# Latent attention by pairs of heads: keys and weighted values of two heads side by side in the array, weights scaled before their transposes

## The chip, the core and the metric

The kernel runs on one core of a Trainium2 chip. Five engines work there from instruction queues of their own: TensorE (PE in the profile, its weight loads PEld), VectorE (DVE), ScalarE (ACT), GpSimd (POOL) and SyncE (SP), which here only issues transfers. The metric is the device time of one launch in microseconds, as the median of several runs. Below, a *bank* is one of the 8 parts of PSUM, the memory that TensorE writes its products to; each holds 512 float32 columns on 128 partitions.

## The reference, cut to what matters

The model has two layers over 256 context tokens and 512 latent tokens of width 1024. Each layer joins three mixers (mLSTM, RWKV-7 and latent attention), projects their output, adds, normalises, and ends in a large lookup of single-neuron experts (PEER). Only the latent attention and the output projection are touched:

```python
def _mla_prep(p, q_norm_g, q_up, kv_norm_g, kv_up, ang):
    cq, ckv, k_rope = _split(p, [384, 256, 32])
    q  = (_rms(cq, q_norm_g) @ q_up).reshape(b, t, 6, 96)        # 64 plain + 32 rotary
    kv = (_rms(ckv, kv_norm_g) @ kv_up).reshape(b, t, 6, 128)    # 64 key + 64 value
    ...                                                          # rotary part, shared by the heads
    return concat([q_nope, q_rope]), concat([k_nope, k_rope]), v

def _attend(q, k, v):
    s = einsum('bqhd,bkhd->bhqk', q, k) * MLA_SCALE
    pr = softmax(s, axis=-1)
    return einsum('bhqk,bkhd->bqhd', pr, v)
```

Latent queries attend to all 768 tokens, context queries to the 256 context tokens; in the last layer context queries are not needed. Then `y = concat([mlstm, rwkv, attention]) @ w_out`.

## The kernel before

Tokens are handled in 6 tiles of 128: tiles 0 and 1 are context, 2 to 5 latent. A plain float32 `nc.tensor.matmul` shows in the trace as two weight loads and two matmuls; the projections use three float32r products of high and low halves instead (`PASSES`).

*Order.* The program is written as Python generators. `weave` advances two or three of them in proportion to given numbers of steps; `flight(units, 3, 2)` keeps up to three units alive, starts a new one every second round, and advances the oldest first. From the order so written and from estimates of its own, the tile framework fixes one list of instructions for each engine before the run. An instruction may be moved ahead of earlier ones on its engine when its inputs are estimated to be there sooner. All tiles from `self.bank()` share one ring of 8 banks.

*Around the attention.* `mixer` first runs `project_mla` (compressed queries `cq` and keys `ckv`, the sums for their norms, and the rotary part of the keys). Then it weaves `mla` (84 steps) with `project_mlstm` (44 steps), whose matmuls are L446 (`fm`, called for each feature tile) and L530. After that come mLSTM and the RWKV projections, then RWKV (whose `tile_prep` has L893), then `project_out`, which is the first step of `peer`.

*`mla`, L744 to L836.* First `rk`, the norm of the keys spread over 64 partitions (L753, L754). Then for each of 6 heads the keys: for both token spans (256 and 512 columns) two accumulated matmuls with 64 weight columns (L760) and a multiplication by `rk` on DVE into `kT` (L761); and for each of 6 token tiles the values `vM` (L764, L765). Then the units: `queries(h)` projects one head's queries for all tokens (L784 to L788, whose last step is on POOL). `unit(h, t)` is one head and one tile of queries, in four steps: scores per span (L799) and their maximum (L800); negated scaled maximum (L804, L805), exponentials with their sums (L809), sum and reciprocal (L811, L812); transposes of the weights (L818) and their copies to SBUF (L820 on DVE, L822 on ACT); weighted values (L826: weights as the stationary operand, the 64 value columns moving), evicted by ACT with the reciprocal as scale (L827). With `need` (layer 0) there are 36 units, 12 of them context tiles over 256 keys; in layer 1 there are 24. With head 5 the row block of a tile goes to DRAM (L829).

*`project_out`, L1198 to L1243.* For each token tile the 1024 features of `y` are loaded, transposed in two groups of four (L1228), and split into high and low halves (L1231 on ACT, L1232 on DVE) for the product with `w_out` (L1239).

Of the kernel before, what the change touches and what calls it, by code (L numbers as in the profile page):

```python
# [20 lines left out]
AF = mybir.ActivationFunctionType  # L21
ALU = mybir.AluOpType
# [6 lines left out]
NT = 6  # L29
NTOK = 768  # L30
# [179 lines left out]
class Net:  # L210
# [533 lines left out]
    def mla(self, p, o):  # L744
# [1 line left out]
        up = self.param(p, l, ("k_up", [128, 2, 384]), ("v_up", [128, 2, 384]))  # L746
        kup, vup = up["k_up"], up["v_up"]

        rk = self.t(p, [64, NTOK], "rk")
        for c, n in TSPANS:  # L750
            ps = self.bank()
            for t in range(n // 128):
                nc.tensor.matmul(ps[:64, t * 128:(t + 1) * 128], lhsT=o["rms"][:, 1, c // 128 + t:c // 128 + t + 1].to_broadcast([128, 64]), rhs=self.ident, start=True, stop=True)  # L753
            nc.scalar.activation(out=rk[:, c:c + n], in_=ps[:64, :n], func=AF.Copy)  # L754
        yield
        for h in range(6):
            for c, n in TSPANS:
                ps = self.bank()
                for i in range(2):
                    nc.tensor.matmul(ps[:64, :n], lhsT=kup[:, i, h * 64:(h + 1) * 64], rhs=o["ckv"][:, i, c:c + n], start=i == 0, stop=i == 1)  # L760
                nc.vector.tensor_tensor(out=self.kT[0:64, h, c:c + n], in0=ps[:64, :n], in1=rk[:, c:c + n], op=ALU.mult)  # L761
            ps = self.bank()
            for i in range(2):
                nc.tensor.matmul(ps[:, :384], lhsT=o["ckv"][:, i, h * 128:(h + 1) * 128], rhs=vup[:, i, :], start=i == 0, stop=i == 1)  # L764
            nc.scalar.activation(out=self.vM[:, h, :], in_=ps[:, :384], func=AF.Copy, scale=o["rms"][:, 1, h:h + 1])  # L765
            yield
        sc = self.t(p, [128, NT], "srq")
        nc.vector.tensor_scalar_mul(out=sc, in0=o["rms"][:, 0, :], scalar1=MLA_SCALE)
        qTs = {}
        yM = self.t(p, [128, NT, 384], "yM")  # L770

        def queries(h):
            qT = self.t(p, [96, NTOK], "qT", 2)
            t1 = self.t(p, [128, NTOK], "rt", 2)
            t2 = self.t(p, [128, NTOK], "rt", 2)
            qup = self.t(p, [128, 3, 128], "q_up", 2)
            nc.sync.dma_start(out=qup, in_=a["q_up"][l, :, :, h * 128:(h + 1) * 128])
            for c, n in TSPANS:
                if c == 0 and not self.need:
                    continue  # L780
                cs = slice(c, c + n)
                ps = self.bank()
                for i in range(3):
                    nc.tensor.matmul(ps[:, :n], lhsT=qup[:, i, :], rhs=o["cq"][:, i, cs], start=i == 0, stop=i == 2)  # L784
                nc.scalar.activation(out=qT[0:64, cs], in_=ps[0:64, :n], func=AF.Copy)
                nc.vector.tensor_tensor(out=t1[64:96, cs], in0=ps[64:96, :n], in1=self.rope[64:96, cs], op=ALU.mult)
                nc.vector.tensor_tensor(out=t2[64:96, cs], in0=ps[96:128, :n], in1=self.rope[96:128, cs], op=ALU.mult)
                nc.gpsimd.tensor_tensor(out=qT[64:96, cs], in0=t1[64:96, cs], in1=t2[64:96, cs], op=ALU.add)  # L788
            qTs[h] = qT
            yield  # L790

        def unit(h, t):
# [17 lines left out]
            if len(spans) == 2:  # L810
                nc.vector.tensor_tensor(out=sm[:, 0:1], in0=sm[:, 0:1], in1=sm[:, 1:2], op=ALU.add)  # L811
            nc.vector.reciprocal(out=sm[:, 0:1], in_=sm[:, 0:1])  # L812
            yield
            pT = self.t(p, [128, NTOK], "pT", 2)
            for c0, w in spans:
                ps = self.bank()
                for i in range(0, w, 128):
# [3 lines left out]
                else:  # L821
                    nc.scalar.activation(out=pT[:, c0:c0 + w], in_=ps[:, :w], func=AF.Copy)  # L822
            yield
            po = self.bank()
            for i in range(nk):
                nc.tensor.matmul(po[:, :64], lhsT=pT[:, i * 128:(i + 1) * 128], rhs=self.vM[:, i, h * 64:(h + 1) * 64], start=i == 0, stop=i == nk - 1)  # L826
            nc.scalar.activation(out=yM[:, t, h * 64:(h + 1) * 64], in_=po[:, :64], func=AF.Copy, scale=sm[:, 0:1])  # L827
            if h == 5:
                nc.sync.dma_start(out=self.y[t * 128:(t + 1) * 128, 640:1024], in_=yM[:, t, :])  # L829

        units = [queries(0)]
        for h in range(6):
            units += [unit(h, t) for t in range(0 if self.need else CT, NT)]
            if h < 5:
                units.insert(len(units) - 2, queries(h + 1))
        yield from self.flight(units, 3, 2)  # L836


# [359 lines left out]
    def project_out(self, p, pw, l, need, xk, hold):  # L1198
# [18 lines left out]
        for s, tiles in streams:  # L1217
            gate = self.gate_rows(p, l, 2, s, f"gate{s}")
            for t in tiles:
# [2 lines left out]
                if left:  # L1222
                    ahead.append(load())
                yT = [self.t(p, [128, 8, 128], f"yT{i}", 2, F32R) for i in range(2)]
                for g in range(2):
                    ps = self.bank()
                    for k in range(4):
                        nc.tensor.transpose(ps[:, k * 128:(k + 1) * 128], y[:, (g * 4 + k) * 128:(g * 4 + k + 1) * 128], self.ident)  # L1228
                    ps = ps.rearrange("p (k n) -> p k n", k=4)
                    hi, lo = (z[:, g * 4:g * 4 + 4, :] for z in yT)  # L1230
                    nc.scalar.activation(out=hi, in_=ps, func=AF.Copy)  # L1231
                    nc.vector.tensor_tensor(out=lo, in0=ps, in1=hi.bitcast(F32), op=ALU.subtract)  # L1232
                z = self.t(p, [128, D], "z", 1)
# [537 lines left out]
```

## Time and profile before

| | |
|---|---|
| median of 3 runs | 5154.06 us (5148.3 to 5161.02) |
| the profiled execution | 5153.65 us, of which its span 5151.7 us |
| busy share of the span | PE 89%, PEld 75%, DVE 71%, POOL 40%, ACT 36% |
| granted TensorE clock, mean | 0.941 of full speed |
| DMA, mean | 192 GB/s |

Rows of the profile read as follows. L818 is line 818 of the kernel. A timeline row gives the start in us from the span's start, how long the instruction or run of like instructions lasted, the engine, the line, the operation, the tile written and those read, and shapes; a bracket at its end tells how long the engine sat idle before it and what it then waited for. A run of matmuls counts from the first start to the last end; matmuls are pipelined, so the next may start before that end. [...]

### The profile page before, as it was taken

What the parts mean: (1) busy time and instruction counts of PE and PEld (TensorE: products, weight loads), DVE (VectorE), ACT (ScalarE), POOL (GpSimd) and SP (SyncE); (2) the same over time, 40 slices, a digit from 0 to 9 for tenths busy, and PEclk for the clock granted to TensorE, in tenths of its full rate; (3) what the DMA queues carried; (4) which work ended last, traced back from release to release, by engine and by line L of the source; (5) the groups of instructions that cost most, each with busy time, mean ns of one, the idle gap of its engine ahead of it and who ended that gap; (6) DMA issues with size and microseconds to landing.
All of it is one profiled execution on the core that took longest, in us unless ns stands there. A gap on an engine that the chain in (4) does not pass through costs nothing.

```text
span 5151.7 us, 89696 instructions
## 1 busy us (share of the span) xinstructions
PE 4604.4 (89%) x35473; PEld 3857.8 (75%) x35473; DVE 3676.4 (71%) x7469; ACT 1848.1 (36%) x3330; POOL 2065.0 (40%) x1761
## 2 busy tenths in 40 slices
PE   6998888888987999999999689978778889999998
PEld 4675567667876887778878467767667888988887
DVE  4444455679885999999999734545579757777777
ACT  2342255232553222222222223345433543333332
POOL 1102333244773555555555210233336634444442
PEclk9998889999998999999999898989989999999999
DMA  4016400321477999999999310100222578999994
GB/s 144 22 43 220 159 4 5 122 83 56 170 284 255 352 342 329 347 342 343 346 335 339 104 34 23 45 22 3 85 96 91 214 269 311 320 316 316 315 319 173
DMA packets 402933, 991.60 MB, mean 192 GB/s; under 512 B 35104, under 2 KB 167584, under 8 KB 401744
## 3 DMA queue, kind: packets, MB, share of 16 engines
q1 hardware_dynamic: 289552, 574.91, 32.2%
q0 software_dynamic: 112960, 410.96, 22.1%
q8 instruction: 279, 4.57, 0.4%
q14 instruction: 142, 1.16, 0.1%
HBM read 894.45 MB, written 91.19 MB: 191 GB/s over the span
## 4 chain that ended last, share of the span: by engine, by line
PE 64%; DVE 15%; POOL 6%; DMA 5%; issue 5%; ACT 4%; SPq 1%; POOLq 0%; DVEq 0%; ACTq 0%
PE acc L1564 17%; PE A L1497 15%; PE b L446 6%; PE b L1355 4%; PE spill L1564 3%; PE b L1497 2%; PE b L1239 2%; DMA c<-early 1%; PE b L799 1%; PE b L1479 1%; PE b L826 1%; PE b L530 1%; DVE py L1617 1%; POOL eq L1430 1%; DMA ut<-in_u_t 1%
## 5 line engine op out<-in xcount | busy, mean ns | idle before, releaser
L1601 POOL DMA_INDIRECT rows<-in_u,eid x384 | 538.3, 1402 | 565.6 <-DVE act L1613 251.8
L1601 POOL DMA_INDIRECT rows<-in_v,eid x384 | 517.0, 1346 | 559.2 <-DVE py L1617 324.4
L1564 PE MATMUL acc<-vhi,clo 128*128 128x512 f32 x1536 | 600.8, 391 | 0.0
L1564 PE MATMUL acc<-vt,chi 128*128 128x512 f32 x1536 | 600.5, 391 | 0.0
L1564 PE MATMUL acc<-vhi,chi 128*128 128x512 f32 x1536 | 599.1, 390 | 0.0
L1497 PE MATMUL A<-hh,uhi 128*128 128x384 f32 (+1 forms) x1472 | 541.1, 368 | 25.5 <-ACT uhi L1266 22.7
L1497 PE MATMUL A<-hh,ut 128*128 128x384 f32 (+1 forms) x1472 | 540.1, 367 | 12.5 <-DVE ut L1267 12.5
L1497 PE MATMUL A<-hl,uhi 128*128 128x384 f32 (+1 forms) x1472 | 540.4, 367 | 0.0
L1266 ACT ACTIVATE uhi<-ut 128x1024 fp32r<-128x1024 f32 x256 | 271.1, 1059 | 629.7 <-PE A L1497 521.7
L1617 DVE SCALAR_TENSOR_TENSOR py<-rows,act,py 128x1024 f32<-128x1024 f32 x381 | 492.4, 1292 | 1.9
L1613 DVE CUSTOM_DVE_ANT_0 rows<-rows,hrow 128x1024 f32<-128x1024 f32 x384 | 463.7, 1240 | 12.2 <-DMA rows<-in_u,eid 12.2
L1266 ACT ACTIVATE vhi<-vt 128x1024 fp32r<-128x1024 f32 x256 | 270.8, 1058 | 555.0 <-PE spill L1564 334.6
L446 PE MATMUL b<-hT,winhi 128*128 128x512 f32 (+1 forms) x1360 | 382.3, 372 | 6.7 <-ACT winhi L1266 4.8
L1267 DVE TENSOR_TENSOR ut<-ut,uhi 128x1024 fp32r<-128x1024 f32 x212 | 275.5, 1299 | 119.6 <-ACT uhi L1266 77.7
L1564 PEld LDWEIGHTS acc<-vhi,clo 128*128 128x128 f32 x1536 | 288.8, 188 | 61.2 <-DVE clo L1253 0.3
L1564 PEld LDWEIGHTS acc<-vhi,chi 128*128 128x128 f32 x1536 | 289.0, 188 | 59.0 <-ACT chi L1252 0.3
L1564 PEld LDWEIGHTS acc<-vt,chi 128*128 128x128 f32 x1536 | 289.0, 188 | 58.9
L1497 PEld LDWEIGHTS A<-hh,uhi 128*128 128x128 f32 x1472 | 278.3, 189 | 62.9 <-ACT uhi L1266 23.5
L1497 PEld LDWEIGHTS A<-hh,ut 128*128 128x128 f32 x1472 | 278.6, 189 | 47.1 <-DVE ut L1267 14.1
L1267 DVE TENSOR_TENSOR vt<-vt,vhi 128x1024 fp32r<-128x1024 f32 x256 | 312.2, 1220 | 1.5 <-PE spill L1564 0.6
L1497 PEld LDWEIGHTS A<-hl,uhi 128*128 128x128 f32 x1472 | 278.5, 189 | 36.1
L446 PEld LDWEIGHTS b<-hT,winhi 128*128 128x128 f32 x1360 | 245.9, 204 | 64.7 <-issue 26.1
(544 smaller groups left out, 10560.7 us busy)
## 6 DMA issues: line engine op xcount, KB each, us to landing
ut<-in_u_t SPq DMA_DIRECT2D x256, 512.0 KB
vt<-in_v SPq DMA_DIRECT2D x256, 512.0 KB
gates<-stage SPq DMA_DIRECT2D x112, 512.0 KB
wmod<-in_w_mod SPq DMA_DIRECT2D x160, 256.0 KB
gt<-gates SPq DMA_DIRECT2D x32, 1024.0 KB
win<-in_w_in SPq DMA_DIRECT2D x52, 512.0 KB
gt<-gates SPq DMA_DIRECT2D x32, 768.0 KB
wq<-in_w_q SPq DMA_DIRECT2D x32, 512.0 KB
```

Source lines behind the costliest of these rows:

```text
L446: self.nc.tensor.matmul(ps[:, :n], lhsT=w[u][:, k, :], rhs=self.hT[v][:, k, c:c + n], start=k + u + v == 0, stop=k == KT - 1 and u == 1)
L530: nc.tensor.matmul(pss[t // 2 * 2][:, t % 2 * 256:t % 2 * 256 + 256], lhsT=self.hT[u][:, j * 4 + k, t * 128:(t + 1) * 128], rhs=wi[v][:, k ...
L799: nc.tensor.matmul(ps[:, :w], lhsT=qTs[h][:, t * 128:(t + 1) * 128], rhs=self.kT[:, h, c0:c0 + w], start=True, stop=True)
L1239: nc.tensor.matmul(ps, lhsT=yT[u][:, k, :], rhs=ws[k][v][:, cs], start=k + u + v == 0, stop=k == KT - 1 and u == 1)
L1266: self.nc.scalar.activation(out=hi, in_=x, func=AF.Copy)
L1267: lo_eng.tensor_tensor(out=lo, in0=x, in1=hi.bitcast(F32), op=ALU.subtract)
L1355: nc.tensor.matmul(ps[:, :n], lhsT=(wh, wl)[x][:, k, :], rhs=(hi, lo)[y][:, k, :], start=k + x + y == 0, stop=k == KT - 1 and x == 1)
L1497: nc.tensor.matmul(bank[:, :n], lhsT=us[x][:, k, :], rhs=(hi, lo)[y][:, k, :], start=k + x + y == 0, stop=k == KT - 1 and x == 1)
L1564: nc.tensor.matmul(b, lhsT=cs[x][:, t * 128:(t + 1) * 128], rhs=vs[y][:, h * 512:(h + 1) * 512], start=s0 and x + y == 0, stop=s1 and x == 1)
L1601: nc.gpsimd.indirect_dma_start(out=r, out_offset=None, in_=a[tab], in_offset=bass.IndirectOffsetOnAxis(ap=eid[:, i:i + 1], axis=0))
L1613: nc.vector.tensor_tensor_reduce(out=r, in0=r, in1=h, scale=1.0, scalar=0.0, op0=ALU.mult, op1=ALU.add, accum_out=act[:, i:i + 1])
L1617: nc.vector.scalar_tensor_tensor(out=y, in0=r, scalar=act[:, i:i + 1], in1=y, op0=ALU.mult, op1=ALU.add)
```

## The change

Four things change, three in `mla` and one in `project_out`.

- Keys: `rk` is spread over 128 partitions, and the keys of two heads come from one matmul with 128 weight columns; two DVE multiplications bring the upper and the lower 64 partitions to `kT`. In each of the 6 steps one pair and one span is done instead of one head and both spans. `rk` takes a buffer of the tag `rt`.
- Softmax: the exponentials are multiplied by the reciprocal of their sum on POOL, in place, before the transposes, where the reciprocal was the scale of the eviction (L827).
- Weighted values: units go by pairs of heads over the same query tile. The first of a pair ends after its transposes. The second does both: the values of each head are the stationary operand (64 columns, each head in its half of the array), the transposed weights move (128 columns), and one bank gets the result with features on partitions (128 features by 128 queries). One ACT copy evicts a pair. `qT` has four buffers instead of two, and two `queries` stand ahead of each pair.
- Output: the attention's third of `y` lies in DRAM with features on partitions. `project_out` transposes only five feature blocks and splits the other three straight from SBUF, in groups of 4, 1 and 3 blocks.

```diff
@@ -746,19 +746,22 @@
         up = self.param(p, l, ("k_up", [128, 2, 384]), ("v_up", [128, 2, 384]))
         kup, vup = up["k_up"], up["v_up"]
 
-        rk = self.t(p, [64, NTOK], "rk")
+        rk = self.t(p, [128, NTOK], "rt", 2)
         for c, n in TSPANS:
             ps = self.bank()
             for t in range(n // 128):
-                nc.tensor.matmul(ps[:64, t * 128:(t + 1) * 128], lhsT=o["rms"][:, 1, c // 128 + t:c // 128 + t + 1].to_broadcast([128, 64]), rhs=self.ident, start=True, stop=True)
-            nc.scalar.activation(out=rk[:, c:c + n], in_=ps[:64, :n], func=AF.Copy)
+                nc.tensor.matmul(ps[:, t * 128:(t + 1) * 128], lhsT=o["rms"][:, 1, c // 128 + t:c // 128 + t + 1].to_broadcast([128, 128]), rhs=self.ident, start=True, stop=True)
+            nc.scalar.activation(out=rk[:, c:c + n], in_=ps[:, :n], func=AF.Copy)
         yield
         for h in range(6):
-            for c, n in TSPANS:
-                ps = self.bank()
-                for i in range(2):
-                    nc.tensor.matmul(ps[:64, :n], lhsT=kup[:, i, h * 64:(h + 1) * 64], rhs=o["ckv"][:, i, c:c + n], start=i == 0, stop=i == 1)
-                nc.vector.tensor_tensor(out=self.kT[0:64, h, c:c + n], in0=ps[:64, :n], in1=rk[:, c:c + n], op=ALU.mult)
+
+            c, n = TSPANS[h % 2]
+            ps = self.bank()
+            for i in range(2):
+                nc.tensor.matmul(ps[:, :n], lhsT=kup[:, i, h // 2 * 128:(h // 2 + 1) * 128], rhs=o["ckv"][:, i, c:c + n], start=i == 0, stop=i == 1)
+            for e in range(2):
+                r = slice(e * 64, e * 64 + 64)
+                nc.vector.tensor_tensor(out=self.kT[0:64, h // 2 * 2 + e, c:c + n], in0=ps[r, :n], in1=rk[r, c:c + n], op=ALU.mult)
             ps = self.bank()
             for i in range(2):
                 nc.tensor.matmul(ps[:, :384], lhsT=o["ckv"][:, i, h * 128:(h + 1) * 128], rhs=vup[:, i, :], start=i == 0, stop=i == 1)
@@ -767,10 +770,11 @@
         sc = self.t(p, [128, NT], "srq")
         nc.vector.tensor_scalar_mul(out=sc, in0=o["rms"][:, 0, :], scalar1=MLA_SCALE)
         qTs = {}
-        yM = self.t(p, [128, NT, 384], "yM")
+        yM = self.t(p, [128, NT, 3, 128], "yM")
+        pTs = {}
 
         def queries(h):
-            qT = self.t(p, [96, NTOK], "qT", 2)
+            qT = self.t(p, [96, NTOK], "qT", 4)
             t1 = self.t(p, [128, NTOK], "rt", 2)
             t2 = self.t(p, [128, NTOK], "rt", 2)
             qup = self.t(p, [128, 3, 128], "q_up", 2)
@@ -810,8 +814,10 @@
             if len(spans) == 2:
                 nc.vector.tensor_tensor(out=sm[:, 0:1], in0=sm[:, 0:1], in1=sm[:, 1:2], op=ALU.add)
             nc.vector.reciprocal(out=sm[:, 0:1], in_=sm[:, 0:1])
-            yield
-            pT = self.t(p, [128, NTOK], "pT", 2)
+            w = sum(w for _, w in spans)
+            nc.gpsimd.tensor_scalar_mul(out=pr[:, :w], in0=pr[:, :w], scalar1=sm[:, 0:1])
+            yield
+            pT = pTs[h] = self.t(p, [128, NTOK], "pT", 2)
             for c0, w in spans:
                 ps = self.bank()
                 for i in range(0, w, 128):
@@ -821,18 +827,23 @@
                 else:
                     nc.scalar.activation(out=pT[:, c0:c0 + w], in_=ps[:, :w], func=AF.Copy)
             yield
+            if h % 2 == 0:
+                return
+
             po = self.bank()
             for i in range(nk):
-                nc.tensor.matmul(po[:, :64], lhsT=pT[:, i * 128:(i + 1) * 128], rhs=self.vM[:, i, h * 64:(h + 1) * 64], start=i == 0, stop=i == nk - 1)
-            nc.scalar.activation(out=yM[:, t, h * 64:(h + 1) * 64], in_=po[:, :64], func=AF.Copy, scale=sm[:, 0:1])
+                for e in range(2):
+                    nc.tensor.matmul(po[e * 64:e * 64 + 64, :128], lhsT=self.vM[:, i, (h - 1 + e) * 64:(h + e) * 64], rhs=pTs[h - 1 + e][:, i * 128:(i + 1) * 128], start=i == 0, stop=i == nk - 1)
+            nc.scalar.activation(out=yM[:, t, h // 2, :], in_=po[:, :128], func=AF.Copy)
             if h == 5:
-                nc.sync.dma_start(out=self.y[t * 128:(t + 1) * 128, 640:1024], in_=yM[:, t, :])
-
-        units = [queries(0)]
-        for h in range(6):
-            units += [unit(h, t) for t in range(0 if self.need else CT, NT)]
-            if h < 5:
-                units.insert(len(units) - 2, queries(h + 1))
+                nc.sync.dma_start(out=self.y[t * 128:(t + 1) * 128, 640:1024], in_=yM[:, t].rearrange("p i n -> p (i n)"))
+
+        units = [queries(0), queries(1)]
+        for h in range(0, 6, 2):
+            units += [unit(h + e, t) for t in range(0 if self.need else CT, NT) for e in range(2)]
+            if h < 4:
+                units.insert(len(units) - 4, queries(h + 2))
+                units.insert(len(units) - 2, queries(h + 3))
         yield from self.flight(units, 3, 2)
 
 
@@ -1222,12 +1233,15 @@
                 if left:
                     ahead.append(load())
                 yT = [self.t(p, [128, 8, 128], f"yT{i}", 2, F32R) for i in range(2)]
-                for g in range(2):
-                    ps = self.bank()
-                    for k in range(4):
-                        nc.tensor.transpose(ps[:, k * 128:(k + 1) * 128], y[:, (g * 4 + k) * 128:(g * 4 + k + 1) * 128], self.ident)
-                    ps = ps.rearrange("p (k n) -> p k n", k=4)
-                    hi, lo = (z[:, g * 4:g * 4 + 4, :] for z in yT)
+
+                for g, n in ((0, 4), (4, 1), (5, 3)):
+                    ps = y[:, 640:1024]
+                    if g < 5:
+                        ps = self.bank()[:, :n * 128]
+                        for k in range(n):
+                            nc.tensor.transpose(ps[:, k * 128:(k + 1) * 128], y[:, (g + k) * 128:(g + k + 1) * 128], self.ident)
+                    ps = ps.rearrange("p (k n) -> p k n", k=n)
+                    hi, lo = (z[:, g:g + n, :] for z in yT)
                     nc.scalar.activation(out=hi, in_=ps, func=AF.Copy)
                     nc.vector.tensor_tensor(out=lo, in0=ps, in1=hi.bitcast(F32), op=ALU.subtract)
                 z = self.t(p, [128, D], "z", 1)
```

## Rows read from the trace of the kernel before

**Rows 1.** Page: busy time of the engines; the chain that ended last, by engine.

```profile
PE 4604.4 (89%) x35473; PEld 3857.8 (75%) x35473; DVE 3676.4 (71%) x7469; ACT 1848.1 (36%) x3330; POOL 2065.0 (40%) x1761
...
PE 64%; DVE 15%; POOL 6%; DMA 5%; issue 5%; ACT 4%; SPq 1%; POOLq 0%; DVEq 0%; ACTq 0%
```

**Rows 2.** Windows: keys and values, units, of layer 0, then layer 1; columns in the first line.

```profile
core 0: us, PE busy (x) PEld busy (x) DVE busy (x) ACT busy (x) POOL busy (x), PEclk, DMA share, GB/s
128.50:171.10 42.60, 41.26 (x144) 22.75 (x144) 10.73 (x20) 7.28 (x13) 2.93 (x2) 0.94 0.04 12
171.10:372.40 201.30, 185.88 (x1106) 151.97 (x1107) 98.75 (x247) 81.25 (x221) 24.61 (x34) 0.94 0.09 29
2990.00:3041.50 51.50, 41.33 (x146) 22.80 (x146) 16.01 (x34) 10.64 (x16) 3.15 (x5) 0.90 0.08 25
3041.50:3216.40 174.90, 159.13 (x878) 127.02 (x879) 77.97 (x194) 60.91 (x162) 16.61 (x23) 0.87 0.07 21
```

**Rows 3.** Timeline, all engines, one unit over 768 keys, layer 1.

```profile
3090.92 1.51 PE L799 MATMUL b<-kT,qT 96*128 96x256 f32 x4
...
3094.20 0.77 ACT L809 ACTIVATE csq<-b,mx,srq 128x512 f32<-128x512 f32 x1
...
3094.38 0.42 PE L818 MATMUL b<-consts_g,csq 128*128 128x128 f32 x2
...
3094.86 0.20 ACT L809 ACTIVATION_READ_ACCUMULATOR csq<-b,mx,srq 128x1 f32 x1
...
3095.11 0.66 PE L818 MATMUL b<-consts_g,csq 128*128 128x128 f32 x4 [0.32 <-ACT csq L809]
...
3095.29 0.16 DVE L812 RECIPROCAL sm<-sm 128x1 f32<-128x1 f32 x1
...
3095.61 0.38 PE L799 MATMUL b<-kT,qT 96*128 96x256 f32 x1
```

**Rows 4.** Timeline, PE: after a long wait in layer 1; last units of layer 0.

```profile
3102.40 1.88 PE L818 MATMUL b<-consts_g,csq 128*128 128x128 f32 x6 [4.04 <-ACT csq L809]
...
3104.06 1.91 PE L799 MATMUL b<-kT,qT 96*128 96x256 f32 x3
...
359.24 2.76 PE L799 MATMUL b<-kT,qT 96*128 96x256 f32 x4
361.80 1.57 PE L826 MATMUL b<-vM,pT 128*128 128x64 f32 x12
364.32 0.44 PE L818 MATMUL b<-consts_g,csq 128*128 128x128 f32 x2 [0.95 <-ACT csq L809]
...
365.67 0.63 PE L799 MATMUL b<-kT,qT 96*128 96x256 f32 x1
```

**Rows 5.** Windows: the unit of rows 3, and the one from 3104.06.

```profile
3090.92:3095.61 4.69, 4.37 (x24) 3.17 (x24) 1.76 (x6) 2.28 (x8) 0.27 (x1) 1.00 0.00 0
3104.06:3109.50 5.44, 5.44 (x15) 3.94 (x15) 2.14 (x6) 1.41 (x4) 0.00 (x0) 0.50 0.00 2
```

**Rows 6.** By line: POOL's tensor-scalar instructions, one operation, then two (ns, shortest/median/longest).

```profile
L557 POOL TENSOR_SCALAR mixed_lo<-pad,p_muc x6: 2212/2619/3689, 386.7 to 3263.3; 128x770 f32<-128x770 f32 x6
...
L509 POOL TENSOR_SCALAR qk<-pad,p_cw,p_cb x8: 983/990/1460, 168.0 to 3128.8; 128x770 f32<-128x770 f32 x8
```

**Rows 7.** Timeline, PE: weighted values, then the like of the RWKV stage.

```profile
3096.90 1.45 PE L826 MATMUL b<-vM,pT 128*128 128x64 f32 x12
...
701.45 0.88 PE L893 MATMUL b<-consts_g,khr 128*64 128x128 f32 x12 [0.90 <-DVE khr L274]
```

**Rows 8.** Groups of instructions: count | busy us, mean ns of one | idle before.

```profile
L826 PE MATMUL b<-vM,pT 128*128 128x64 f32 x624 | 81.8, 281 | 0.3 <-ACT pT L822 0.3
...
L760 PE MATMUL b<-ckv,p_k_up 128*64 128x256 f32 (+1 forms) x96 | 33.5, 492 | 0.0
```

**Rows 9.** By line: output projection, transposes and high halves.

```profile
L1228 PE MATMUL b<-consts_g,ycat x80: 270/273/473, 953.5 to 3756.7; 128*128 128x128 f32 x80
...
L1231 ACT ACTIVATE yT<-b x20: 578/596/600, 955.0 to 3757.1; 128x512 fp32r<-128x512 f32 x20
```

## The prediction

> **What bounds the kernel now.** I read the page first: TensorE (PE) is busy for 89% of the span and holds 64% of the chain that ended last [rows 1]. An average says nothing of one stage, so I went on to the windows over the four stretches that the change touches: keys and values of layer 0, its attention units, and the same two of layer 1 [rows 2]. Together they last 470.3 us, and PE is busy in 427.6 of them. That looks like a stage bound by PE, in which fewer matmul microseconds would be time won.
>
> The timeline of one unit says something else. A unit is one head and one tile of 128 queries. The unit shown starts its scores (L799) at 3090.92 and the next unit starts at 3095.61, 4.69 us later [rows 3]. Follow it: scores of 512 keys on PE, their maximum on VectorE (DVE), negated and scaled there, two exponentials on ScalarE (ACT), the last of which gives up its sum at 3095.06; at 3095.11 PE begins the four last transposes (L818), half a microsecond later the next scores. That is a closed loop. The projections of the mLSTM (L446 here, L530 elsewhere) fill PE inside it, so PE looks busy, but a period is set by the loop and not by the sum of the matmuls. Two rows show that the loop can't be overlapped. PE is idle for 0.32 us before the four transposes, and for 4.04 us before those at 3102.40, though the next unit's scores need only queries and keys that were ready long before [rows 3, 4]. Over all 60 units of the trace (36 in layer 0, 24 in layer 1) no scores stand ahead of the transposes of the unit before; both write PSUM banks of one ring, which are first written in program order.
>
> **The change part by part.** Durations are those of the profiled execution, 5153.65 us long (span 5151.7, the median of the runs 5154.06), and the sum is made against it.
>
> *The weights are scaled before the transposes.* The softmax division moved from the eviction of the output (L827, off the loop) to a multiplication of the whole weight tile on GpSimd (POOL), ahead of the `yield` after which the transposes are traced. So the sum's addition (L811), the reciprocal (L812) and this POOL instruction enter the loop. L812 ends at 3095.45, 0.39 us after the last exponential [rows 3]; today nothing but L827 waits for it. For the POOL instruction the trace has no row, so it is bounded by POOL's other tensor-scalar instructions: with two operations (multiply and add, L509) 770 columns take 0.99 us in most cases, with one operation (multiply alone, L557, four groups of six, the first shown) never under 2.21 us [rows 6]. The new one multiplies alone, so I take 2.21 us for 768 columns; 0.99 stays as the lower end, the 3.69 that L557 reached once as the upper. Two handovers cost 0.05 us each, as from ACT to PE at 3095.06. Last, all six transposes now wait for the end, where two ran between the exponentials: two more at 0.12 us. The loop becomes 4.69 + 0.39 + 2.21 + 0.05 + 0.24 = 7.6 us, 2.9 more. For the 48 units over 768 keys that is +139 us. The 12 units over 256 keys (layer 0's context queries) have 256/768 of the multiplication, about 0.75 us, and a reciprocal of 0.16 [rows 3]; they are shorter loops with some slack in PE, and I take +0.7 each, +8 us. POOL's queue holds little else here (L509, L516, L788; 41 us in the two unit stretches together [rows 2]), and behind the waiting multiplication stand only those, which are early today.
>
> [...]
>
> *What cannot pay for it.* PE gets some 2.5 us of idle time a unit: 7.6 less the 4.4 for which it is busy in the unit shown [rows 5], which has no weighted values, and less 0.7 for those of a mean unit after the change. After the 4.04 us gap the next unit ran at half clock: granted clock 0.50, three score matmuls 1.91 us where four took 1.51 [rows 3 to 5]. In layer 0's last units, without filling, gaps of 0.95 and 0.32 us were enough to keep it there: scores 2.76 us, and a period of 6.43 [rows 4]. [...] That lengthens the loop by 1.25 us of scores (2.76 against 1.51) and about 0.3 of transposes, 1.55 a unit. Ten full units run so today, by the length of their scores in the timeline. Ends: none more, or all 38 others (+59 us); I take eight more, +12 us, because at half clock the filling alone would close the gaps and let the clock up again.
>
> *Units where PE was late.* In some eight full units, like that from 3104.06, PE has no gap at all [rows 5] and transposes start up to 2 us after the exponentials. There part of the 2.9 is slack: −10 us.
>
> *Weighted values by pairs (L826).* The same number of instructions, 624 [rows 8], now 64 weight columns wide, two heads in two halves of the array. Today 12 take 1.45 us; the like form in the RWKV stage (L893, 128 by 64, halves in turn, 128 columns) takes 0.88 for 12 [rows 7]. 624/12 × 0.57 = 30 us of PE time. But they lie in the shadow between scores and transposes; in the tail at 361.80 they end well before the 0.95 us gap [rows 4]. They pay only where PE has no gap, mostly the rounds in which a head's queries are projected: a third, −10 us; ends 0 and −30. Changes of the array's division between transposes and these are in L893's row already, which stands between others.
>
> *Keys by pairs (L760).* 96 matmuls become 48 of the same width; DVE's multiplications keep count and size (64 partitions, two for one). All 96 are busy for 33.5 us [rows 8]. In that stretch PE is nearly saturated in layer 0 (41.3 of 42.6 us) and has gaps in layer 1 (41.3 of 51.5) [rows 2]: 16.7 us at most, I take −14. The broadcast of the norm (L753) moves 128 columns as before.
>
> *Output projection.* Three of eight transposes a token tile go, 30 of 80 at 0.12 us of PE; ACT and DVE get three copies and subtractions of 512, 128 and 384 columns for two of 512 (0.60 us each on ACT) [rows 9]. A fixed cost more against PE time less, both inside a stage of matmuls: 0, between −4 and +4. L827 halves in count, off the loop. More buffers for queries and the shared buffer of `rk` add no wait: their earlier readers are DVE instructions ahead in the same queue.
>
> Sum: 139 + 8 + 12 − 10 − 10 − 14 = +125 us. The unit stretches end one after the other into the next stage, whose first bank comes after theirs, so I know no cover. Since the two context-size terms and the late units are rough, I round to **5275 us**.
>
> **The rivals.** (a) *The multiplication is quick.* If POOL takes 0.99 us, 48 × 1.22 and a few more are saved: 5153.65 + 125 − 60 = 5218. For it: a plain multiplication should not be dearer than multiply and add. Against it: all four groups of L557. [...]
> (b) *The other side: the loop opens.* If the new wait makes the order put the next unit's scores ahead of these transposes, the POOL time is hidden, PE becomes the bound, and the PE savings count in full: 30 + 14 + 3 = 47 us faster, 5107. It decides as soon as two units overlap in the unit stretches. For it: 8 banks, of which the loop uses five or six. Against it: none of 60 units does so, not even over the 4.04 us gap.
> (c) *The filling hides it.* If idle PE time draws the projections forward, they end sooner, and the query rounds have less beside them; if that gave back as much as the loop takes, the time would stay about 5150. Against it: the filling in all 48 loops is in the shadow already (PE is busy for 4.37 of 4.69 us in the one shown [rows 5]).
> (d) *The halves do not run side by side.* Then the weighted values cost PE 1.45 us for 12 as before, and the 10 us of that term go: 5285.
>
> **How the numbers follow.** My forecast (with d inside it) has 0.77; (a) 0.10, (b) 0.08, (c) 0.05. The forecast alone spans 5240 (no cold unit more, some slack) to 5340 (all cold, and 2.6 us on POOL, the median of the group shown). The range takes in (a) and leaves (b), (c) and the far cold end: 5205 to 5325. A measurement of this kernel can tell about 0.3%, 15 us, from no change: slower by more than that 0.87, the same 0.05, faster 0.08.
>
> **What would show it.** Periods of 7.4 to 9.3 us from L799 to L799 in units over 768 keys; a POOL row of 48 or more multiplications at about 2.2 us; L818 waiting for POOL and no longer for ACT; a lower granted clock in both unit stretches; L760 at half its busy time and L826 at about 0.07 us an instruction. Periods near 6.3 would be (a); scores of the next unit ahead of transposes, (b). I am wrong as a whole if the unit stretches don't get longer.

## The result, and the profile after

The changed kernel takes 5303.9 us (median of 4 runs, 5297.6 to 5313.16), the kernel before beside it 5155.5: 148.4 us more, a ratio of 1.029 with an interval of 1.0275 to 1.0304. The profiled execution took 5297.6 us, of which its span 5295.7, 144.0 more than the span of before. The time lies in the forecast range, 29 us above the 5275 us; the sum of +125 is some 23 us short.

First the page of the changed kernel, engines and chain, as [rows 1]:

```profile
PE 4596.9 (87%) x35395; PEld 3834.5 (72%) x35395; DVE 3680.0 (69%) x7479; ACT 1844.5 (35%) x3310; POOL 2184.3 (41%) x1821
...
PE 62%; DVE 15%; POOL 9%; issue 5%; ACT 5%; DMA 4%; SPq 1%; POOLq 0%; DVEq 0%; ACTq 0%
```

PE is no busier than before and the span is longer; the chain that ended last lost 2 points on PE and gained 3 on POOL. Where that happens, the windows over the same four stretches as in [rows 2] tell (keys and values, units; layer 0, then layer 1):

```profile
core 0: us, PE busy (x) PEld busy (x) DVE busy (x) ACT busy (x) POOL busy (x), PEclk, DMA share, GB/s
128.40:166.20 37.80, 37.35 (x144) 26.38 (x145) 14.37 (x26) 9.01 (x16) 5.57 (x7) 0.93 0.08 23
166.20:463.40 297.20, 192.91 (x1071) 141.33 (x1069) 96.96 (x240) 76.49 (x200) 86.32 (x66) 0.78 0.06 18
3081.80:3123.80 42.00, 36.44 (x141) 25.25 (x141) 16.10 (x35) 11.15 (x17) 3.19 (x5) 0.92 0.12 36
3123.80:3365.80 242.00, 160.38 (x884) 116.93 (x885) 84.65 (x195) 59.50 (x151) 71.10 (x46) 0.78 0.05 16
```

The units grew by 96 us in layer 0 and 67 in layer 1, the keys shrank by 5 and 9.5. PE's idle time in the two stretches of units rose from 31 us to 186, and its granted clock fell from 0.94 and 0.87 to 0.78; it was busy for 353.3 us, 8 longer, with fewer matmuls. Everything else in the span is within 6 us of before. The median instructions of DVE and ACT in these stretches are not slower beside the busier POOL (each kind within 0.01 us of before or quicker, the maximum over 512 columns 0.692 us in both), so the loss is not slower work on these two. One unit of layer 1, all engines, shows the loop as [rows 3] did:

```profile
3218.44 1.46 PE L803 MATMUL b<-kT,qT 96*128 96x256 f32 x4
...
3221.67 0.77 ACT L813 ACTIVATE csq<-b,mx,srq 128x512 f32<-128x512 f32 x1
...
3222.33 0.20 ACT L813 ACTIVATION_READ_ACCUMULATOR csq<-b,mx,srq 128x1 f32 x1
...
3222.56 0.16 DVE L815 TENSOR_TENSOR sm<-sm 128x1 f32<-128x1 f32 x1 [1.54 <-ACT csq L813]
3222.75 0.16 DVE L816 RECIPROCAL sm<-sm 128x1 f32<-128x1 f32 x1
3223.11 2.20 POOL L818 TENSOR_SCALAR csq<-csq,sm 128x768 f32<-128x768 f32 x1 [5.43 <-DVE sm L816]
...
3225.37 0.88 PE L824 MATMUL b<-consts_g,csq 128*128 128x128 f32 x6 [3.13 <-POOL csq L818]
...
3226.08 2.71 PE L803 MATMUL b<-kT,qT 96*128 96x256 f32 x4
```

The next scores start 7.64 us after these. The sum, the reciprocal and the multiplication, which nothing on PE waited for before, stand between the last exponential (end 3222.53) and the transposes (3225.37), and the next unit's scores came out at half clock: 2.71 us for four matmuls that took 1.46 one unit earlier (granted clock 0.51 in 3226.08:3228.79, 1.00 in 3218.44:3226.08). In the last units of layer 0, where the mLSTM projections have run out, every unit is like that (PE alone, granted clock 0.50 in 441.81:445.92, cf. [rows 4]):

```profile
441.81 1.54 PE L824 MATMUL b<-consts_g,csq 128*128 128x128 f32 x6 [5.54 <-POOL csq L818]
443.15 2.77 PE L803 MATMUL b<-kT,qT 96*128 96x256 f32 x4
445.85 2.41 PE L836 MATMUL b<-pT,vM 128*64 128x128 f32 x24
452.25 1.54 PE L824 MATMUL b<-consts_g,csq 128*128 128x128 f32 x6 [4.00 <-POOL csq L818]
```

The waits of PE in layer 1's units (us in total, times, longest):

```profile
PE b L824 <- POOL csq L818: 81.6, 24, 7.5
```

The rows by line of the multiplication, the paired weighted values and the paired keys (ns: shortest/median/longest), then the last two by groups as in [rows 8], then one pair's weighted values on PE's timeline:

```profile
L818 POOL TENSOR_SCALAR csq<-csq,sm x60: 923/2205/2219, 170.4 to 3362.6; 128x768 f32<-128x768 f32 x48, 128x256 f32<-128x256 f32 x12
...
L836 PE MATMUL b<-pT,vM x624: 272/273/476, 176.5 to 3369.9; 128*64 128x128 f32 x156
...
L761 PE MATMUL b<-ckv,p_k_up x48: 377/486/592, 134.6 to 3111.4; 128*128 128x256 f32 x24, 128*128 128x512 f32 x24
```

```profile
L836 PE MATMUL b<-pT,vM 128*64 128x128 f32 x624 | 48.0, 306 | 0.0
...
L761 PE MATMUL b<-ckv,p_k_up 128*128 128x256 f32 (+1 forms) x48 | 17.4, 485 | 0.0
```

```profile
3212.65 1.53 PE L836 MATMUL b<-pT,vM 128*64 128x128 f32 x24
```

All 24 units of layer 1 wait for POOL, 81.6 us in total; one multiplication takes 2.205 us, where L557, one operation too, took 2.21 at its shortest [rows 6]. The keys are 48 matmuls where [rows 8] had 96. In none of the 59 successions of units do scores start ahead of the transposes of the unit before.

### The profile page after: what moved, and what is told of

The parts are those of the page before. It is cut to its first block, busy times and chain, and to the rows that moved or that the text cites. A ratio compares the mean times of both kernels' runs of the same rounds, so it can differ in the third digit from the quotient of the medians.

```text
span 5295.7 us, 89643 instructions
## 1 busy us (share of the span) xinstructions
PE 4596.9 (87%) x35395; PEld 3834.5 (72%) x35395; DVE 3680.0 (69%) x7479; ACT 1844.5 (35%) x3310; POOL 2184.3 (41%) x1821
## 4 chain that ended last, share of the span: by engine, by line
PE 62%; DVE 15%; POOL 9%; issue 5%; ACT 5%; DMA 4%; SPq 1%; POOLq 0%; DVEq 0%; ACTq 0%
PE acc L1578 17%; PE A L1511 15%; PE b L446 5%; PE b L1369 4%; PE spill L1578 3%; POOL csq L818 2%; PE b L1511 2%; PE b L803 2%; PE b L1493 1%; PE b L1253 1%; ACT csq L813 1%; POOL eq L1444 1%; PE b L824 1%; DMA c<-early 1%; DMA ut<-in_u_t 1%
```

## The experiments

Differences are between medians, each against the kernel before run beside it (5149 to 5156 us). "Period" is the median from one unit's scores to the next one's within a layer, over the units of 768 keys whose score matmuls kept PE busy for up to 2 us; "cold" counts those of the 48 whose score matmuls kept it busy for longer, and the others are called warm; "open" counts the successions (of 59) in which the next scores start ahead of the transposes; the clock is the granted one in the units of layers 0 and 1.

| kernel | us | against before | interval of the ratio | period | cold | open | clock |
|---|---|---|---|---|---|---|---|
| before | 5155.5 | | | 5.28 | 10 | 0 | 0.94, 0.87 |
| changed | 5303.9 | +148.4 | 1.0275 to 1.0304 | 8.26 | 23 | 0 | 0.78, 0.78 |
| e10: before + multiplication | 5317.2 | +164.9 | 1.0301 to 1.0336 | 8.18 | 19 | 0 | 0.80, 0.80 |
| e1: changed − multiplication | 5119.2 | −32.8 | 0.9926 to 0.9959 | 5.06 | 6 | 0 | 0.91, 0.90 |
| e8: before + keys by pairs | 5135.4 | −14.0 | 0.9964 to 0.9986 | 5.28 | 10 | 0 | 0.92, 0.87 |
| e2: two operations on POOL | 5239.2 | +87.2 | 1.0146 to 1.0182 | 6.81 | 20 | 0 | 0.83, 0.81 |
| e3: multiplication on DVE | 5195.6 | +43.6 | 1.0069 to 1.0102 | 6.55 | 15 | 0 | 0.89, 0.86 |
| e12: scores repeated in the gap | 5203.9 | +51.6 | 1.0082 to 1.0116 | 6.24 | 4 | 25 | 0.95, 0.97 |
| e4: changed, scores first | 5171.9 | +19.9 | 1.0021 to 1.0047 | 6.02 | 2 | 50 | 0.91, 0.94 |
| e5: before, scores first | 5107.4 | −42.0 | 0.9905 to 0.9932 | 4.64 | 1 | 48 | 0.99, 0.97 |
| e6: division on the result | 5122.5 | −26.8 | 0.9931 to 0.9958 | 5.04 | 4 | 0 | 0.95, 0.90 |
| e7: e6, scores first | 5095.1 | −54.3 | 0.9880 to 0.9910 | 5.46 | 0 | 50 | 0.95, 0.99 |
| e11: e5 + keys by pairs | 5090.9 | −61.4 | 0.9869 to 0.9902 | 4.65 | 1 | 48 | 0.98, 0.97 |
| e9: e7, sums by head and tile | 5077.0 | −75.3 | 0.9839 to 0.9872 | 4.73 | 0 | 50 | 0.98, 0.96 |

### One part alone: multiplication, pairs, keys

The multiplication put into the kernel before, and taken out of the changed one:

```diff
 # e10, on the kernel before
+            w = sum(w for _, w in spans)
+            nc.gpsimd.tensor_scalar_mul(out=pr[:, :w], in0=pr[:, :w], scalar1=sm[:, 0:1])
...
-            nc.scalar.activation(out=yM[:, t, h * 64:(h + 1) * 64], in_=po[:, :64], func=AF.Copy, scale=sm[:, 0:1])
+            nc.scalar.activation(out=yM[:, t, h * 64:(h + 1) * 64], in_=po[:, :64], func=AF.Copy)
 # e1, on the changed kernel
-            w = sum(w for _, w in spans)
-            nc.gpsimd.tensor_scalar_mul(out=pr[:, :w], in0=pr[:, :w], scalar1=sm[:, 0:1])
```

> The kernel before with one part of the change alone: the multiplication of the weights on GpSimd ahead of the transposes, and an eviction without a scale; no pairs. Theory (the multiplication costs what the changed kernel shows beside the same kernel without it, 185 us, and the pairs give their 33 independently of it): 5152 + 185 = 5337 us, 5320 to 5355, period of a unit up by 3.0 us. Rival (part of the 185 comes from the pairs with the multiplication, such as the longer order of units or two heads' buffers): 5280 to 5310.

> The changed kernel without the multiplication on GpSimd; the weights stay undivided, so this leaves out the division by the sum. Theory (the multiplication and the wait for the reciprocal, 0.4 + 0.2 + 2.2 us, lengthen a closed loop of 48 units): the period of a unit over 768 keys falls from 7.64 us to 4.6 to 5.0, the cold units go back to about ten, L824 waits for ScalarE again, and the time is 5154 less the keys (14) and the weighted values (0 to 30): 5105 to 5140 us. Rival 1 (something else in the change costs: halves of the array, the layout of the result, the order of the units): the time stays above 5200. Rival 2 (the cold clock is the loss by itself, and the change of unit order brings it): the period falls but some 24 units stay cold, about 5170.

Alone it costs 165 us; without it (e1, which leaves the division out) the rest of the change is 33 us faster than before. So the loss is the multiplication and what it does to the loop, and rival 1 of e1 (halves, layout or order cost) falls. The two prices differ: 181 us from e1 to the changed kernel, 165 in e10. The cold units, 17 more in the one and 9 more in the other, would account for that at the 2.0 us each that they are counted at below, but no run sets the clock alone. e10 lies between its band of 5320 to 5355 and the rival's of 5280 to 5310; the pairs are worth 33 us without the multiplication and 16 with it. The windows over e10's units show the same as those of the changed kernel:

```profile
171.20:475.00 303.80, 212.15 (x1106) 170.65 (x1106) 99.36 (x246) 80.67 (x221) 88.25 (x70) 0.80 0.06 19
3151.80:3391.40 239.60, 175.63 (x909) 138.63 (x910) 81.39 (x194) 61.07 (x164) 71.16 (x47) 0.80 0.05 16
```

They are 102 and 65 us longer than in [rows 2], at nearly the same low clock, without any pairs.

e8 makes the keys by pairs on the kernel before, as in the diff above (`rk` on 128 partitions, L756 to L764).

> The kernel before with the keys by pairs of heads alone (48 matmuls in place of 96). Theory (half of the 33.5 us of L760 goes where TensorE has few gaps): 10 to 17 us less, 5137 to 5144. Rival (the stretch is bound by something else, VectorE or the banks): within 6 us of 5154.

14.0 us less, interval 7 to 19: the term as forecast.

### The length of the wait

```diff
 # e2, e3, on the changed kernel
-            nc.gpsimd.tensor_scalar_mul(out=pr[:, :w], in0=pr[:, :w], scalar1=sm[:, 0:1])
+            nc.gpsimd.tensor_scalar(out=pr[:, :w], in0=pr[:, :w], scalar1=sm[:, 0:1], scalar2=0.0, op0=ALU.mult, op1=ALU.add)   # e2
+            nc.vector.tensor_scalar_mul(out=pr[:, :w], in0=pr[:, :w], scalar1=sm[:, 0:1])   # e3
```

> The changed kernel with the same multiplication on GpSimd written with two operations (times the reciprocal, plus 0.0). Theory (the loop pays every microsecond of the instruction, and with two operations it takes 0.99 us as L509 did): the row of L818 falls from 2.2 to about 1.0 us, the period of a unit over 768 keys from 7.64 to 6.4, and with 48 times 1.2 and fewer cold units the time is 5215 to 5245 us. Rival 1 (two operations are no quicker on this tile, L509's rows owe it to their operands): row and time as in the changed kernel, about 5300. Rival 2 (the instruction is quicker, but something else is late next): row at 1.0 us, time above 5270.

> The changed kernel with the multiplication on VectorE in place of GpSimd. Theory (length of the instruction and handovers in the loop are what counts, whatever the engine): about 0.6 us an instruction by L515 on VectorE, and the handover from the reciprocal on the same engine goes; period 5.7 to 6.1 us, 48 times 1.6 to 1.9 us less than the changed kernel and some ten cold units fewer: 5180 to 5215 us. Rival (VectorE is full, and the multiplication stands in its queue in front of the maxima of the next unit or behind evictions): above 5240.

Both times lie within their bands; the periods, 6.81 and 6.55 us, lie above the 6.4 and the 5.7 to 6.1 expected from the one unit of 7.64 (the median of the changed kernel is 8.26). Rows by line of e2, then of e3:

```profile
L818 POOL TENSOR_SCALAR csq<-csq,sm x60: 478/906/1161, 169.4 to 3307.4; 128x768 f32<-128x768 f32 x48, 128x256 f32<-128x256 f32 x12
```

```profile
L818 DVE TENSOR_SCALAR csq<-csq,sm x60: 347/620/623, 170.0 to 3257.3; 128x768 f32<-128x768 f32 x48, 128x256 f32<-128x256 f32 x12
```

The same multiplication of the same tile takes 0.91 us on POOL instead of 2.21 when it also adds zero; that is L509 against L557 in [rows 6] again. 1.3 us less in 48 units makes 62, and 61 were measured. That is closer than it should be: the 12 context units (0.45 us each) and three cold units fewer would add some 11. On DVE it takes 0.62, and the median handover from the reciprocal is 0.03 us instead of 0.19, though that to PE is 0.15 instead of 0.05. Every tenth of a microsecond in the loop is paid some fifty times.

Between 256 and 768 columns (shortest and median) e2's rows grow by 0.84 ns a column, the changed kernel's one-operation rows by 2.5 ns, three times that.

### Opening the loop

e4 and e5 change one line of `flight` for the attention's units, in the changed kernel and in the kernel before: within a round the newest unit is advanced first, so that the scores of the next unit are written ahead of the transposes.

```diff
-            for g in list(live):
+            for g in (live[::-1] if newest else list(live)):
```

> The changed kernel with the units in flight advanced newest first, so that the scores of the next unit stand ahead of the transposes of the unit before on TensorE; the multiplication on GpSimd stays at 2.2 us. Theory (it is the closed loop that makes the latency cost, and not the work added): while the multiplication runs, TensorE has the next unit's scores, the period falls from 7.64 us to about 4.5 to 5.5, bound by TensorE or by the chain of one unit shared by two, and the time is 5100 to 5160 us. Rival (the latency is paid wherever the scores stand, since banks or buffers close the loop elsewhere): the period stays above 6.5, 5250 or more.

> The kernel before with the units in flight advanced newest first; nothing else is changed. Theory (the kernel before is held by the same closed loop, with only some 40 us of gaps on TensorE in the two unit stretches, since the projections fill it): 10 to 40 us less, 5115 to 5145. Rival (the gaps of the kernel before are filled by projections that the next stage would otherwise do, and TensorE is the bound): within 8 us of 5154.

e4 takes back 128 of the 148 us with the multiplication as slow as ever, so the closed loop is a large part of what the latency costs. It is not all of it. Opening the loop gains 42 us where there is no multiplication (e5), and beside e9, which has the same order and divides elsewhere, e4 is 95 us slower, over half of the 181 from e1 to the changed kernel. It misses its band by 12 us, its period is 6.0 us where I expected at most 5.5, and PE still waits. Its windows over the units, and PE's waits in layer 1's, where the changed kernel had 24 and 81.6 us:

```profile
167.50:390.00 222.50, 176.70 (x1071) 133.53 (x1069) 95.65 (x240) 75.43 (x200) 87.04 (x66) 0.91 0.08 24
3065.00:3240.80 175.80, 136.62 (x859) 101.47 (x859) 82.30 (x195) 58.51 (x150) 70.35 (x45) 0.94 0.07 21
```

```profile
PE b L824 <- POOL csq L818: 39.1, 17, 7.5
```

All engines of e4 show one wait that is new:

```profile
3215.84 2.20 POOL L818 TENSOR_SCALAR csq<-csq,sm 128x768 f32<-128x768 f32 x1 [4.40 <-DVE mx L809]
...
3217.40 0.16 DVE L815 TENSOR_TENSOR sm<-sm 128x1 f32<-128x1 f32 x1 [0.60 <-ACT csq L813]
3218.10 0.88 PE L824 MATMUL b<-consts_g,csq 128*128 128x128 f32 x6 [2.03 <-POOL csq L818]
...
3219.01 0.69 DVE L826 COPY pT<-b 128x512 f32<-128x512 f32 x1 [1.45 <-PE b L824]
...
3219.62 0.15 DVE L816 RECIPROCAL sm<-sm 128x1 f32<-128x1 f32 x1
...
3219.97 2.20 POOL L818 TENSOR_SCALAR csq<-csq,sm 128x768 f32<-128x768 f32 x1 [1.92 <-PE b L803]
```

The first multiplication, the transposes and the copy are of one unit, the rest of the next. Its sum is ready at 3217.56, but on DVE its reciprocal stands behind the copy (L826) of transposes that wait for POOL. That is a new wait, in DVE's queue, 2.1 us from sum to reciprocal here. But only 4 of the 48 units have it for over 1.5 us; in the median unit the reciprocal follows its sum by 0.03 us, so it explains little of the miss. What is longer in most is the whole chain: in warm units the reciprocal ends 6.4 us after the scores' start (median), 4.6 in the changed kernel. Which queue adds most of this is not shown.

e5 is the kernel before with nothing but its loop opened: 42 us faster, more than I had expected. So the stretches of units in the kernel before were held by this loop too, although PE was busy for 92% of them [rows 2]:

```profile
170.70:353.70 183.00, 176.55 (x1107) 144.92 (x1107) 96.02 (x246) 82.26 (x221) 25.85 (x34) 0.99 0.10 30
3020.60:3176.10 155.50, 146.78 (x873) 117.53 (x874) 78.21 (x194) 60.68 (x162) 19.56 (x22) 0.97 0.08 24
```

They are 38 us shorter, 16 of it PE's idle time and 22 its busy time, at a granted clock of 0.99 and 0.97 instead of 0.94 and 0.87.

e12 was meant for the clock. It repeats the scores in the banks of the transposes while POOL multiplies:

```diff
 # e12, on the changed kernel
+            pts = [self.bank() for _ in spans]
+            for ps, (c0, w) in zip(pts, spans):
+                if len(spans) == 2:
+                    nc.tensor.matmul(ps[:, :w], lhsT=qTs[h][:, t * 128:(t + 1) * 128], rhs=self.kT[:, h, c0:c0 + w], start=True, stop=True)
...
-                ps = self.bank()
```

> The changed kernel with work added to TensorE: in every unit over 768 keys the scores are computed a second time, into the banks that the transposes overwrite, while GpSimd multiplies. 48 times 1.46 us more for TensorE, none of it behind a wait that the loop has not got. Theory (the gaps let the clock fall, and 23 cold units pay 2.0 us each against 6 without the multiplication): the cold units fall to ten or fewer and the time by 20 to 45 us, to 5260 to 5285. Rival 1 (the clock is not set by these gaps): still some 23 cold units, and with 1.46 or 2.77 us more work 5300 to 5360. Rival 2 (the gap is filled, but the mLSTM projections that ran there now come later): cold units fewer, 5290 to 5330.

None of the three: 5203.9 us, 100 less than the changed kernel, with 48 score products more. PE's timeline shows why (L803 scores, L824 here the repeated ones; the transposes, L827, come later):

```profile
363.02 1.56 PE L824 MATMUL b<-kT,qT 96*128 96x256 f32 x4
364.42 1.45 PE L803 MATMUL b<-kT,qT 96*128 96x256 f32 x4
```

The next unit's scores run behind the repeated ones and ahead of the transposes, in 25 successions, though units are still advanced oldest first. The first writer of the transposes' banks no longer waits for POOL, and so the next banks' writers may follow it. That supports the reading of the prediction that the ring's order of first writers closed the loop. But it is no test of the clock: cold units fell from 23 to 4, and the run doesn't tell how much of the 100 us is theirs.

### A version without the wait

e6 divides the result instead of the weights. Two small matmuls a pair spread the reciprocals over the columns of the same bank, one ACT copy takes 256 columns, and POOL multiplies 128 by 128, behind nothing that the loop needs. e7 adds the order of e4; there the reciprocal of a pair's first head was overwritten by that of the following tile, for which the spread waited, so e7 divides by another tile's sum. e9 keeps them apart. e11 is e5 with the keys by pairs.

```diff
 # e6, on the changed kernel, which also drops the multiplication
+            for e in range(2):
+                nc.tensor.matmul(po[e * 64:e * 64 + 64, 128:256], lhsT=sms[h - 1 + e][:, 0:1].to_broadcast([128, 64]), rhs=self.ident, start=True, stop=True)
...
-            nc.scalar.activation(out=yM[:, t, h // 2, :], in_=po[:, :128], func=AF.Copy)
+            yr = self.t(p, [128, 256], "yr", 2)
+            nc.scalar.activation(out=yr, in_=po[:, :256], func=AF.Copy)
+            nc.gpsimd.tensor_tensor(out=yM[:, t, h // 2, :], in0=yr[:, :128], in1=yr[:, 128:256], op=ALU.mult)
 # e9, on e7
-                nc.tensor.matmul(po[e * 64:e * 64 + 64, 128:256], lhsT=sms[h - 1 + e][:, 0:1].to_broadcast([128, 64]), rhs=self.ident, start=True, stop=True)
+                nc.tensor.matmul(po[e * 64:e * 64 + 64, 128:256], lhsT=sms[h - 1 + e, t][:, 0:1].to_broadcast([128, 64]), rhs=self.ident, start=True, stop=True)
```

> The changed kernel with the division moved off the loop: two matmuls a pair spread the reciprocals over the columns, one ScalarE copy of 256 columns takes result and reciprocals out, and GpSimd multiplies the two, 128 by 128. Theory (the division costs only where it stands between exponentials and transposes): period 4.6 to 5.0 us, time as without the multiplication plus 0 to 10 us, 5105 to 5150. Rival (the spread of the reciprocals, 60 more matmuls of 0.1 us, and longer ScalarE copies come into the path): 5160 to 5200.

> Division off the loop and scores ahead of the transposes, both in one kernel. Theory (loop open and PE the bound, savings of keys and weighted values count in full): 5085 to 5125 us, lower than either alone. Rival (one of the two is enough, TensorE is the bound with either): equal to the lower of the two within 8 us.

> Division on the result, off the loop, and scores ahead of the transposes, each reciprocal kept under its own head and tile. Theory (loop open and TensorE the bound): 5090 to 5100 us, about 12 below the kernel before with its scores first. Rival (the ratio of the earlier kernel of this form hung on its data, or the order is worth nothing beside the division): 5115 to 5125 as with the division moved alone.

> The kernel before with scores first and the keys by pairs, weighted values head by head as before. Theory (once the loop is open, TensorE is the bound, and the 35 us of TensorE time that the paired weighted values save count in full): keys give 14 of 5107, so 5093, and the kernel with paired values and scores first would have to be some 25 lower, which it is not at 5095; so if this theory is right this kernel is near 5120. Rival (paired values save TensorE time that is not on the path even then): 5088 to 5098, equal to the paired kernel.

e6 is 27 us faster than before: the division costs only where it stands in the loop. e9 is the fastest kernel, 75 us below before, and lower than I had expected. Its windows over the units:

```profile
165.80:340.90 175.10, 163.49 (x1139) 127.51 (x1137) 93.74 (x240) 76.76 (x200) 31.37 (x46) 0.98 0.10 31
3003.70:3141.90 138.20, 131.56 (x893) 101.10 (x893) 77.42 (x194) 58.02 (x149) 23.29 (x32) 0.96 0.09 27
```

PE is busy for 94% of these, at a granted clock of 0.98 and 0.96. Against e11, which has the keys and the open loop but weighs the values head by head, e9 is 14 us faster, the price of its spread included. My expectation for e11 had set it against e7's 5095. Its 5090.9 lies in the rival's band, but e7 had a wait of its own, and beside e9 the rival is weaker: the paired form pays in an open loop, though less than the 37 us by which PE is less busy with weighted values (83.1 against 46.0). That the weighted values alone bring the 14 us is not shown, since the order of the units and the output projection differ too. e7 to e9 is 21 us, each against its own base, 13 of them in the two stretches of units.

## Why the prediction came out as it did

- *The loop* (+139). Right. POOL 2.205 us against 2.21 [rows 6]; the reciprocal ends 0.39 after the last exponential, as forecast; the warm period of the unit shown is 7.64 against 7.6. In the median of warm units the last transpose starts 3.51 us after the last exponential, before 0.47: 3.04 instead of 2.9, since the handover from DVE to POOL took 0.19 us and not 0.05. 48 units: +146.
- *Context units* (+8). POOL 0.93 us instead of 0.75; the last transpose ends 1.0 us later in the mean: +12.
- *Half clock* (+12). The term that was mis-sized. 13 more units were cold, not 8, and one cost 2.0 us (median periods 10.25 and 8.26), not 1.55: scores 2.77 against 1.46, six transposes 1.54 against 0.87, where I had counted 0.3. That makes +26. The price is counted from rows; no run here changed the clock alone. In the trace of before, gaps of 0.95 and 0.32 us did not keep the clock down: around the unit of 359.24 [rows 4] it was 1.00 in 356:358, 0.50 in 359:362 and 0.98 in 362:363, with no mLSTM matmul there. Behind the unit of 3104.06, which ran without a gap at 0.50 [rows 5], it was 1.00 in 3110.5:3127; that the filling does this and so holds the cold units to eight more, as I had reasoned, no run tests.
- *Late PE* (−10). The last exponential of warm units ends 4.19 us after the scores' start, 4.40 before: about 0.2 a unit, 10 in 48. That is not the slack of the eight late units that I had in mind, so the agreement with the 10 forecast is luck.
- *Weighted values* (−10). 24 instructions of a pair take 1.53 us where two times 12 took 1.45 each [rows 7]: 0.064 us each, 0.07 was forecast, and 34 us of PE time went (81.8 [rows 8] against 48.0), 30 forecast. With the multiplication in place the pairs give 16.5 us, of which the keys alone 14: little was left, and 23 units were cold against e10's 19. That these four took most of the 10 us back fits the sizes (4 times 2.0) but is not shown. Without the multiplication the pairs give 19 us beside the keys.
- *Keys* (−14): −14.0. *Output projection* (0): the span behind layer 1's units is 5 us shorter, but it is so in e5 too, which leaves the projection alone; no gain of it is shown.

With the three terms that changed, the sum is 146 + 12 + 26 − 10 − 10 − 14 = 150, against 148 by the medians and 144 by the spans. The mechanism was right: the loop, the half clock and the keys carry it. That the sum comes this close is partly luck, since two of its terms of −10 are kept as forecast and not measured.

The rivals. (a), a quick multiplication, is excluded by its row, and e2 shows that its price was right: 61 us below the changed kernel, 60 forecast. (b), the open loop, didn't happen, and its price was wrong: I took PE as the bound and 5107 us, but e4, which does open it, takes 5172: PE is idle for 85 of the 398 us of its two stretches and waits for POOL in 17 of layer 1's 24 units. (c) falls with the 155 us of new idle time in the units. (d) falls with L836's 1.53 us.

## What to carry to other kernels

Before moving a step such as a division, look which side of the serial chain it lands on: a division that nobody waited for became 3.0 us in each of 48 rounds, and moved to the result it costs 6 us in all (e1 to e6), which is within the noise. A stage in which PE is 92% busy can still be bound by its loop; look for the gap in one period and for the order of first writers in the shared banks, and open the loop before saving matmuls (42 us here for one line). When the granted clock is lower behind a gap on PE, charge that to scores and transposes alike: at 0.50 here the four score matmuls took 2.77 us and not 1.46, the six transposes 1.54 and not 0.87.

## What the runs showed of the hardware

A tensor-scalar multiplication on POOL over 128 by 768 float32 took 2.205 us with one operation (changed kernel) and 0.906 with two (times a column, plus zero; e2), in the median; over 256 columns 0.923 and 0.478 at the shortest. On DVE the one-operation form took 0.620, and 0.347 at the shortest (e3). With 64 weight columns in alternate halves of the array, 24 float32 matmuls of 128 moving columns took 1.53 us (changed kernel, at 3212.65); 24 with 128 weight columns and 64 moving took two times 1.45 (before [rows 7]).
